# RWKV-7 layer on one core: key-query products on four array quarters, state outputs behind the chain of states, output stage in two parts

## Chip, cores and metric

The kernel runs on one core of a Trainium2 chip. The metric is the device time of one execution in microseconds (us); the time given for a kernel is the median of its runs. The core has TensorE (PE in the rows; PEld is its weight load), VectorE (DVE), ScalarE (ACT), GpSimd (POOL) and SyncE (SP), each with a queue of its own that it works off in order.

## The reference, cut to what matters

Two layers. The first mixes tokens with RWKV-7 heads (12 heads of 64, 2048 tokens), the second with differential attention; both attend to 256 memory tokens beside that, and an output projection follows each. The change is in the first layer alone, in this recurrence and what surrounds it:

```python
def step(state, inp):
    r_t, w_t, k_t, v_t, kk_t, a_t = inp
    sa = jnp.einsum('bhvk,bhk->bhv', state, -kk_t)
    state = (state * w_t[:, :, None, :]
             + sa[..., None] * (kk_t * a_t)[:, :, None, :]
             + v_t[..., None] * k_t[:, :, None, :])
    y_t = jnp.einsum('bhvk,bhk->bhv', state, r_t)
    return state, y_t
...
y = ((y - mean) * lax.rsqrt(var + LNX_EPS)).reshape(B, S, BR_W) * lnx_w + lnx_b
bonus = jnp.sum(r * k * r_k, axis=-1, keepdims=True) * v
return y + bonus.reshape(B, S, BR_W)
```

The caller multiplies the result by a SiLU gate.

## The kernel before

The recurrence is computed in chunks of 64 tokens. A step takes one pair of heads (128 columns) and a block of 512 tokens, which is eight chunks. There are 24 steps: two halves of the tokens, six pairs of heads, two blocks. The methods of a step:

- `p1`: the projections of the pair (`pj`, 24 matmuls of 128x128x512 each, for the keys kx, the receptances rx and the values vx, L174), the decay and its running sum (two `lr` products for the decay cum and two for asg, L317 and L318), the token shift (`mix`, three VectorE operations, L277 to L279), and the norm of the keys (`pss`, L335, which needs kk from kx).
- `p2`: key-query products `pg` (L371) of each chunk and head, masked into Gm (L373); transposes `bkp` and `pvt`; the bonus.
- `p3`: VectorE inverts 16x16 and 32x32 blocks of a triangular matrix by substitution (itmp and Ti alternate, L418 and L420), brings them with stream transposes into T and TT (L427, L431). `p3b`: TensorE doubles the blocks (`inv` L446, `invz` L459, `invr` L465).
- `gate`: projection and SiLU of the gate (L282 to L288).
- `p4`: the products that give each chunk's transition matrix MT and the rest (`atp`, `nvp`, `txp`, `mrp`, and `ch<-UV,BKT` L530).
- `p4b`: the chain of states. Eight links `ch<-S,MT` (L541), each followed by a copy to S on ScalarE (L542), which the next link reads; the first reads the state sb of the block before. The outputs `yp` come in part from inside a chunk (L550) and in part from the state (L555), two matmuls to a chunk, each of which needs that chunk's S.
- `p5`: VectorE normalises ys (bn_stats bs L564, a few small operations sm, L574 and L575), TensorE transposes it (`py`, L578), ScalarE scales (L580), VectorE adds the bonus (L581), GpSimd gates (L582) and stores to y_dram (L583).

The program is written in the order of a software pipeline: in turn i it holds p2 and p3 of step i+1, p4b and p5 of step i, p3b and p4 of step i+1, and then the gate of step i+1 and p1 of step i+2. A scheduler takes this program and sets the order of instructions on each engine, so pj of a later step stands between the links of the chain and in other places as a filler. The PSUM pool for pg, bkp, yp, py and the inverses has three buffers that go round; pj has three of its own.

Of the kernel before, what the change touches and what calls it, by code (L numbers as in the profile page):

```python
# [59 lines left out]
def hybrid_kernel(ctx, tc, S, HALF, x, mem, pv, cv, dist, postn, w_out, w_mkv, a_w, w2, a2, w_kv, b_w, out):  # L60
# [148 lines left out]
    def layer_a(ph):  # L209
# [64 lines left out]
        def mix(ps, col, o):  # L274
            m = pc("mu", col)
            A.activation(o, ps, AF.Copy, scale=omu[:, col:col + 1])
            V.scalar_tensor_tensor(out=o[:, 1:TB], in0=ps[:, 0:TB - 1], scalar=m, in1=o[:, 1:TB], op0=ALU.mult, op1=ALU.add)  # L277
            V.scalar_tensor_tensor(out=o[:, 0:1], in0=carry[:, col:col + 1], scalar=m, in1=o[:, 0:1], op0=ALU.mult, op1=ALU.add)
            V.tensor_copy(out=carry[:, col:col + 1], in_=ps[:, TB - 1:TB])  # L279

        def gate_silu(ps, g, eng=G_):
            A.activation(g, ps, AF.Copy)  # L282
            e = W([P, TB], "e_sil")
            A.activation(e, g, AF.Exp, scale=-1.0)
            V.tensor_scalar(out=e, in0=e, scalar1=BIG, scalar2=None, op0=ALU.min)
            A.activation(e, e, AF.Ln, bias=1.0)
            A.activation(e, e, AF.Exp, scale=-1.0)
            eng.tensor_tensor(out=g, in0=g, in1=e, op=ALU.mult)  # L288
            return g
# [13 lines left out]
        class Step:  # L303
# [5 lines left out]
            def p1(self):  # L309
# [5 lines left out]
                for i, e in enumerate((cum[:, :, 1:65], asg.rearrange("p (c t) -> p c t", t=C))):  # L315
# [3 lines left out]
                    A.activation(e, pl.rearrange("p (c t) -> p c t", t=C), AF.Exp, bias=nwa[:, i * 6 + p:i * 6 + p + 1], scale=-1.0)  # L319
                    V.tensor_scalar(out=e, in0=e, scalar1=BIG, scalar2=None, op0=ALU.min)  # L320
                    A.activation(e, e, AF.Ln, bias=1.0)
# [40 lines left out]
            def p2(self):  # L362
                p, AR, BK = self.p, self.AR, self.BK
                Gm = T([P, 2, NJ, 2, P], "Gm", 2)
                for e in range(2):

                    pgs = [PS([P, NJ, P], "pg") for hh in range(2)]
                    for j in range(NJ):
                        for hh in range(2):
                            hs = slice(hh * 64, hh * 64 + 64)  # L370
                            mm(pgs[hh][:, j, :], lhsT=BK[hs, 2 * j + e, :], rhs=AR[hs, 2 * j + e, :], start=True, stop=True)  # L371
                    for hh in range(2):
# [160 lines left out]
            def p4b(self):  # L533
# [6 lines left out]
                for c in range(NC):  # L540
                    mm(ch[:, c, :], lhsT=MT[:, c, :], rhs=st[c], start=False, stop=True, skip_group_check=True)  # L541
                    A.activation(st[c + 1], ch[:, c, :], AF.Copy, scale=PC[:, c:c + 1])  # L542
# [3 lines left out]
                for hh in range(2):  # L546
                    for j in range(NJ):
                        for e in range(2):
                            rr = hcs[e]
                            mm(py[hh][rr, j, :], lhsT=Gm[:, e, j, hh, rr], rhs=UV[:, 2 * j + e, hcs[hh]], start=j == 0, stop=False, skip_group_check=True)  # L550
                for j in range(NJ):
                    for e in range(2):
                        for hh in range(2):
                            c, rr = 2 * j + e, hcs[e]
                            mm(py[hh][rr, j, :], lhsT=RT[hcs[hh], c, :], rhs=st[c][hcs[hh]], start=False, stop=True, skip_group_check=True)  # L555
                for hh in range(2):
                    A.activation(ys[:, :, hh], py[hh], AF.Copy)

            def p5(self):
                p, ys, sil = self.p, self.ys, self.sil  # L560
                bs = T([P, 8, 6], "bs", 1)
# [12 lines left out]
                V.tensor_tensor(out=y8, in0=y8, in1=sm[:, 0, :, None].broadcast_to([P, 8, 64]), op=ALU.subtract)  # L574
                V.tensor_tensor(out=y8, in0=y8, in1=sm[:, 3, :, None].broadcast_to([P, 8, 64]), op=ALU.mult)  # L575
                py = PS([P, NJ, P], "py")
                for j in range(NJ):
# [115 lines left out]
        for i in range(n):  # L693
# [11 lines left out]
            if i + 1 < n:  # L705
                steps[i + 1].p3b()
                steps[i + 1].p4()
            if i + 2 <= n:
                filler(i + 2)
# [614 lines left out]
```

## Time and profile before

| what | value |
|---|---|
| median of 3 runs | 3177.18 us (3177.15 to 3179.72) |
| the profiled execution, its own time | 3178.13 us |
| span of the profile | 3176.3 us |
| TensorE busy | 2965.9 us, 93% |
| VectorE, ScalarE, GpSimd busy | 1792.0, 1508.2, 873.6 us |
| mean granted clock of TensorE | 0.97 |

The steps of the first layer run up to about 1480 us of the span. A stretch is the time from the first pg matmul of one step to the first of the next; stretches are counted from 0, and stretch 6 and 7 are shown most below. In rows of a timeline the columns are the start, the time from first start to last end, the engine, line, operation, what it writes and reads, its sizes, how many matmul passes it holds (a 32-bit matmul is recorded as two), and in brackets the engine's idle time before it with what ended it.

### The profile page before, as it was taken

What the parts mean: (1) busy time and instruction counts of PE and PEld (TensorE: products, weight loads), DVE (VectorE), ACT (ScalarE), POOL (GpSimd) and SP (SyncE); (2) the same over time, 40 slices, a digit from 0 to 9 for tenths busy, and PEclk for the clock granted to TensorE, in tenths of its full rate; (3) what the DMA queues carried; (4) which work ended last, traced back from release to release, by engine and by line L of the source; (5) the groups of instructions that cost most, each with busy time, mean ns of one, the idle gap of its engine ahead of it and who ended that gap; (6) DMA issues with size and microseconds to landing.
All of it is one profiled execution on the core that took longest, in us unless ns stands there. A gap on an engine that the chain in (4) does not pass through costs nothing.

```text
span 3176.3 us, 57448 instructions
## 1 busy us (share of the span) xinstructions
PE 2965.9 (93%) x22378; PEld 2401.6 (76%) x22378; DVE 1792.0 (56%) x4728; ACT 1508.2 (47%) x3318; POOL 873.6 (28%) x936
## 2 busy tenths in 40 slices
PE   6889999998789999998899999999999999998999
PEld 4667777776667777777677798898887787786777
DVE  6566767655656676764465311101108888887554
ACT  5535454444444544444455422313216777776343
POOL 3133433442134334431000222412312223222100
PEclk8999999998789999999999999999999999999999
DMA  3211000122110001103554523423454556533453
GB/s 118 80 30 36 28 23 26 35 77 79 36 33 28 23 26 33 38 25 86 164 145 126 155 80 99 118 83 87 117 158 110 114 112 120 116 80 108 121 156 115
DMA packets 266160, 265.45 MB, mean 84 GB/s; under 512 B 16832, under 2 KB 206656, under 8 KB 265760
## 3 DMA queue, kind: packets, MB, share of 16 engines
q1 hardware_dynamic: 237760, 195.31, 21.0%
q0 software_dynamic: 28128, 66.46, 10.3%
q8 instruction: 176, 2.88, 0.4%
q14 instruction: 96, 0.79, 0.1%
HBM read 180.45 MB, written 81.26 MB: 82 GB/s over the span
## 4 chain that ended last, share of the span: by engine, by line
PE 71%; DVE 13%; ACT 8%; issue 3%; DMA 3%; POOL 1%; SPq 1%; ACTq 0%; DVEq 0%; POOLq 0%
PE pj L174 28%; PE po L866 10%; PE o L1179 5%; PE vps L1042 4%; PE s L1138 3%; PE s L1139 2%; PE tr L1169 2%; DMA wraw<-in_a_w 2%; PE inv L446 2%; PE yp L555 1%; PE ch L541 1%; PE mo L805 1%; DVE E L1141 1%; PE mpt L798 1%; PE pss L335 1%
## 5 line engine op out<-in xcount | busy, mean ns | idle before, releaser
L174 PE MATMUL pj<-hhi,wh 128*128 128x512 f32 x928 | 396.3, 427 | 7.8 <-ACT sil L282 2.6
L174 PE MATMUL pj<-hhi,wl 128*128 128x512 f32 x928 | 379.4, 409 | 1.3 <-POOL wl L123 1.3
L174 PE MATMUL pj<-hlo,wh 128*128 128x512 f32 x928 | 373.9, 403 | 0.2 <-DVE hlo L149 0.2
L123 POOL TENSOR_TENSOR wl<-wraw,wh 128x512 fp32r<-128x512 f32 x168 | 220.0, 1320 | 431.5 <-ACT wh L122 378.0
L1141 DVE CUSTOM_DVE_ANT_0 E<-s,dist 128x512 f32<-128x512 f32 (+1 forms) x480 | 276.0, 604 | 35.2 <-PE s L1139 29.0
L174 PE MATMUL pj<-bh,wh 128*128 128x512 f32 x672 | 262.4, 391 | 0.0
L174 PE MATMUL pj<-bh,wl 128*128 128x512 f32 x672 | 262.3, 390 | 0.0
L174 PE MATMUL pj<-bl,wh 128*128 128x512 f32 x672 | 262.2, 390 | 0.0
L1146 ACT ACTIVATE E<-E,nm 128x1920 f32<-128x1920 f32 (+7 forms) x192 | 229.4, 1199 | 59.0 <-DVE nm L1144 58.6
L174 PEld LDWEIGHTS pj<-hhi,wh 128*128 128x128 f32 x928 | 179.2, 193 | 64.7 <-ACT sil L282 8.9
L122 ACT ACTIVATE wh<-wraw 128x512 fp32r<-128x512 f32 x168 | 105.2, 627 | 231.3 <-PE pj L174 143.6
L1179 PE MATMUL o<-th,vs 128*128 128x256 f32 (+1 forms) x864 | 210.9, 376 | 2.4 <-ACT th L1172 0.9
L174 PEld LDWEIGHTS pj<-hlo,wh 128*128 128x128 f32 x928 | 179.7, 194 | 41.7 <-issue 6.8
L174 PEld LDWEIGHTS pj<-hhi,wl 128*128 128x128 f32 x928 | 178.6, 192 | 42.0 <-POOL wl L123 2.2
L1138 PE MATMUL s<-ks,qd 128*128 128x512 f32 (+1 forms) x480 | 205.7, 432 | 2.2 <-DVE mx L1141 1.2
L1179 PEld LDWEIGHTS o<-th,vs 128*128 128x128 f32 x864 | 153.9, 189 | 38.5 <-ACT th L1172 19.2
L1139 PE MATMUL s<-ks,qd 128*128 128x512 f32 (+1 forms) x480 | 176.2, 373 | 0.0
L174 PEld LDWEIGHTS pj<-bh,wh 128*128 128x128 f32 x672 | 126.6, 188 | 26.3 <-DVE ot L877 0.3
L174 PEld LDWEIGHTS pj<-bh,wl 128*128 128x128 f32 x672 | 126.5, 188 | 26.3
L174 PEld LDWEIGHTS pj<-bl,wh 128*128 128x128 f32 x672 | 126.5, 188 | 25.9
L764 POOL DMA_DIRECT2D mq<-mq x64 | 33.3, 526 | 376.0 <-PE ms L783 368.3
L1172 ACT ACTIVATE th<-tr 128x512 f32<-128x512 f32 (+1 forms) x216 | 113.2, 568 | 44.2 <-PE tr L1169 43.8
(416 smaller groups left out, 7112.1 us busy)
## 6 DMA issues: line engine op xcount, KB each, us to landing
wraw<-in_a_w SPq DMA_DIRECT2D x126, 256.0 KB, 2.9
qd<-qd_d POOLq DMA_DIRECT2D x48, 512.0 KB, 7.0
mq<-mq POOLq DMA_DIRECT2D x64, 256.0 KB, 4.3
ks<-ks_d POOLq DMA_DIRECT2D x24, 512.0 KB, 7.2
yr<-y_dram SPq DMA_DIRECT2D x31, 384.0 KB, 5.0
xt<-in_x SPq DMA_DIRECT2D x16, 512.0 KB, 5.3
x_dram<-ot SPq DMA_DIRECT2D x16, 512.0 KB, 4.2
wraw<-in_b_w SPq DMA_DIRECT2D x32, 256.0 KB, 3.1
```

What stands on the lines that cost most here:

```text
L122: A.activation(hi[:, ks], raw, AF.Copy)
L123: eng.tensor_tensor(out=lo[:, ks], in0=raw, in1=hi[:, ks].bitcast(F32), op=ALU.subtract)
L174: mm(ps, lhsT=w[a_][:, k, wcol], rhs=h[b_][:, k, tsl], start=n == 0, stop=n == 3 * KT - 1)
L446: mm(pb[rows, j, hh, :], lhsT=lt[rows, j, hh, :], rhs=rt_[rows, j, hh, :], start=True, stop=True)
L866: mm(po[hf], lhsT=a_[:, k, :], rhs=b_[hf][:, k, :], start=k == i == 0, stop=k == KT - 1 and i == 2)
L1042: mm(ps[:, t, :], lhsT=hT[b][a_][:, k, tsl], rhs=w[b_][:, k, :], start=n == 0, stop=n == 3 * KT - 1)
L1138: mm(ps[:, f:f + w_], lhsT=qd[:, 0, c, qs], rhs=k_[:, c, 0:w_], start=True, stop=False)
L1139: mm(ps[:, f:f + w_], lhsT=qd[:, 1, c, qs], rhs=k_[:, c, 0:w_], start=False, stop=True)
L1141: V.tensor_tensor_reduce(out=e[:, kb * 512:kb * 512 + w], in0=ps[:, 0:w], in1=dt_[:, u0:u0 + w], scale=-SLOPES[h], scalar=3.0e38, op0=ALU. ...
L1146: A.activation(E[c][:, 0:nk], E[c][:, 0:nk], AF.Exp, bias=nm[:, c:c + 1], scale=-1.0, accum_out=nm[:, 2 + c:3 + c])
L1172: A.activation(th[:, 0:w], ps[:, 0:w], AF.Copy)
L1179: mm(po[:, oc], lhsT=vs[kt // 4][:, kt % 4, :], rhs=th[:, rc], start=n == 0, stop=n >= nmm - 2, skip_group_check=True)
```

## The change

Four edits. The key-query products of a chunk and head are split in two by output rows, so each reads 64 key rows, 64 columns of weights, and writes to one of four quarters; there are 32 matmuls where there were 16. The state outputs of a step are issued behind the last matmul of its chain. p5 ends with the normalised ys; transposes, scaling, bonus, gate and store are a method p5b, called between p3b and p4 of the next step (for the last step right behind p5). And the VectorE operations of the token shift, and the clamp in two sigmoids, have high priority for the scheduler.

```diff
--- before.py
+++ after.py
@@ -274,15 +274,17 @@
         def mix(ps, col, o):
             m = pc("mu", col)
             A.activation(o, ps, AF.Copy, scale=omu[:, col:col + 1])
-            V.scalar_tensor_tensor(out=o[:, 1:TB], in0=ps[:, 0:TB - 1], scalar=m, in1=o[:, 1:TB], op0=ALU.mult, op1=ALU.add)
-            V.scalar_tensor_tensor(out=o[:, 0:1], in0=carry[:, col:col + 1], scalar=m, in1=o[:, 0:1], op0=ALU.mult, op1=ALU.add)
-            V.tensor_copy(out=carry[:, col:col + 1], in_=ps[:, TB - 1:TB])
+            with tc.high_priority():
+                V.scalar_tensor_tensor(out=o[:, 1:TB], in0=ps[:, 0:TB - 1], scalar=m, in1=o[:, 1:TB], op0=ALU.mult, op1=ALU.add)
+                V.scalar_tensor_tensor(out=o[:, 0:1], in0=carry[:, col:col + 1], scalar=m, in1=o[:, 0:1], op0=ALU.mult, op1=ALU.add)
+                V.tensor_copy(out=carry[:, col:col + 1], in_=ps[:, TB - 1:TB])
 
         def gate_silu(ps, g, eng=G_):
             A.activation(g, ps, AF.Copy)
             e = W([P, TB], "e_sil")
             A.activation(e, g, AF.Exp, scale=-1.0)
-            V.tensor_scalar(out=e, in0=e, scalar1=BIG, scalar2=None, op0=ALU.min)
+            with tc.high_priority():
+                V.tensor_scalar(out=e, in0=e, scalar1=BIG, scalar2=None, op0=ALU.min)
             A.activation(e, e, AF.Ln, bias=1.0)
             A.activation(e, e, AF.Exp, scale=-1.0)
             eng.tensor_tensor(out=g, in0=g, in1=e, op=ALU.mult)
@@ -317,7 +319,8 @@
                     mm(pl, lhsT=lora[:, i], rhs=th[i], start=True, stop=False)
                     mm(pl, lhsT=lora[:, 2 + i], rhs=th[i], start=False, stop=True)
                     A.activation(e, pl.rearrange("p (c t) -> p c t", t=C), AF.Exp, bias=nwa[:, i * 6 + p:i * 6 + p + 1], scale=-1.0)
-                    V.tensor_scalar(out=e, in0=e, scalar1=BIG, scalar2=None, op0=ALU.min)
+                    with tc.high_priority():
+                        V.tensor_scalar(out=e, in0=e, scalar1=BIG, scalar2=None, op0=ALU.min)
                     A.activation(e, e, AF.Ln, bias=1.0)
                     A.activation(e, e, AF.Exp, scale=-1.0)
                 kx = W([P, TB], "kx")
@@ -366,9 +369,11 @@
 
                     pgs = [PS([P, NJ, P], "pg") for hh in range(2)]
                     for j in range(NJ):
-                        for hh in range(2):
-                            hs = slice(hh * 64, hh * 64 + 64)
-                            mm(pgs[hh][:, j, :], lhsT=BK[hs, 2 * j + e, :], rhs=AR[hs, 2 * j + e, :], start=True, stop=True)
+                        for d in range(2):
+                            for hh in range(2):
+                                o = hh ^ d
+                                hs, os_ = slice(hh * 64, hh * 64 + 64), slice(o * 64, o * 64 + 64)
+                                mm(pgs[hh][os_, j, :], lhsT=BK[hs, 2 * j + e, os_], rhs=AR[hs, 2 * j + e, :], start=True, stop=True)
                     for hh in range(2):
                         V.tensor_tensor(out=Gm[:, e, :, hh, :], in0=pgs[hh], in1=cc(("maskE", "maskO")[e], 128)[:, None, :].broadcast_to([P, NJ, P]), op=ALU.mult)
 
@@ -538,7 +543,7 @@
                 S = T([P, NC, C], "S", 1)
                 st = [sb[self.p][:, b % 2]] + [S[:, c] for c in range(1, NC)] + [sb[self.p][:, 1 - b % 2]]
                 for c in range(NC):
-                    mm(ch[:, c, :], lhsT=MT[:, c, :], rhs=st[c], start=False, stop=True, skip_group_check=True)
+                    last = mm(ch[:, c, :], lhsT=MT[:, c, :], rhs=st[c], start=False, stop=True, skip_group_check=True)
                     A.activation(st[c + 1], ch[:, c, :], AF.Copy, scale=PC[:, c:c + 1])
                 ys = self.ys = T([P, NJ, 2, C], "ys", 1)
 
@@ -548,16 +553,17 @@
                         for e in range(2):
                             rr = hcs[e]
                             mm(py[hh][rr, j, :], lhsT=Gm[:, e, j, hh, rr], rhs=UV[:, 2 * j + e, hcs[hh]], start=j == 0, stop=False, skip_group_check=True)
-                for j in range(NJ):
-                    for e in range(2):
-                        for hh in range(2):
-                            c, rr = 2 * j + e, hcs[e]
-                            mm(py[hh][rr, j, :], lhsT=RT[hcs[hh], c, :], rhs=st[c][hcs[hh]], start=False, stop=True, skip_group_check=True)
+                with tc.issue_after(last.ins):
+                    for j in range(NJ):
+                        for e in range(2):
+                            for hh in range(2):
+                                c, rr = 2 * j + e, hcs[e]
+                                mm(py[hh][rr, j, :], lhsT=RT[hcs[hh], c, :], rhs=st[c][hcs[hh]], start=False, stop=True, skip_group_check=True)
                 for hh in range(2):
                     A.activation(ys[:, :, hh], py[hh], AF.Copy)
 
             def p5(self):
-                p, ys, sil = self.p, self.ys, self.sil
+                ys = self.ys
                 bs = T([P, 8, 6], "bs", 1)
                 y8 = ys.rearrange("p j h v -> p (j h) v")
                 for i in range(8):
@@ -573,6 +579,9 @@
                 A.activation(sm[:, 3], sm[:, 3], AF.Exp, scale=-0.5)
                 V.tensor_tensor(out=y8, in0=y8, in1=sm[:, 0, :, None].broadcast_to([P, 8, 64]), op=ALU.subtract)
                 V.tensor_tensor(out=y8, in0=y8, in1=sm[:, 3, :, None].broadcast_to([P, 8, 64]), op=ALU.mult)
+
+            def p5b(self):
+                p, ys, sil = self.p, self.ys, self.sil
                 py = PS([P, NJ, P], "py")
                 for j in range(NJ):
                     nc.tensor.transpose(py[:, j, :], ys[:, j].rearrange("p h v -> p (h v)"), ident)
@@ -704,7 +713,11 @@
             steps[i].p5()
             if i + 1 < n:
                 steps[i + 1].p3b()
+                if True:
+                    steps[i].p5b()
                 steps[i + 1].p4()
+            if False or i + 1 == n:
+                steps[i].p5b()
             if i + 2 <= n:
                 filler(i + 2)
             if i == n - 2:
```

The built programs show what becomes of the order. TensorE, in the chain of stretch 6 (ch is a link, yp the outputs, pj a filler). Before, from its first link:

```order
L541 MATMUL ch<-sb_122,MT 128x64
L550 MATMUL yp<-UV,Gm 64x64 x16
L555 MATMUL yp<-sb_122,RT 64x64 x2
L541 MATMUL ch<-S,MT 128x64
L555 MATMUL yp<-S,RT 64x64 x2
L174 MATMUL pj<-hhi,wh 128x512
L174 MATMUL pj<-hlo,wh 128x512
L541 MATMUL ch<-S,MT 128x64
L555 MATMUL yp<-S,RT 64x64 x2
L174 MATMUL pj<-hhi,wl 128x512
L541 MATMUL ch<-S,MT 128x64
```

With the change, the end of the same chain:

```order
L546 MATMUL ch<-S,MT 128x64
L174 MATMUL pj<-hhi,wh 128x512
L174 MATMUL pj<-hlo,wh 128x512
L546 MATMUL ch<-S,MT 128x64
L174 MATMUL pj<-hhi,wl 128x512
L174 MATMUL pj<-hhi,wh 128x512
L546 MATMUL ch<-S,MT 128x64
L561 MATMUL yp<-sb_122,RT 64x64 x2
L561 MATMUL yp<-S,RT 64x64 x14
L174 MATMUL pj<-hlo,wh 128x512
L174 MATMUL pj<-hhi,wl 128x512
L174 MATMUL pj<-hhi,wh 128x512
```

The two yp matmuls of a link are gone from between the links, two pj stand in each, and the state outputs come as one block behind the last link.

TensorE at the end of stretch 6, where mrp ends one step's p4 and pss belongs to p1 of a later step. Before:

```order
L519 MATMUL mrp<-BKT,Wn 64x64
L520 MATMUL mrp<-Gm,Wn 64x64
L530 MATMUL ch<-UV,BKT 64x64 x16
L335 MATMUL pss<-rn,cvt 128x512
L174 MATMUL pj<-hhi,wh 128x512
L174 MATMUL pj<-hlo,wh 128x512
L174 MATMUL pj<-hhi,wl 128x512
```

With the change, behind `ch<-UV` and six more pj:

```order
L174 MATMUL pj<-hhi,wl 128x512
L174 MATMUL pj<-hhi,wh 128x512
L174 MATMUL pj<-hlo,wh 128x512
L174 MATMUL pj<-hhi,wl 128x512
L546 MATMUL ch<-sb_124,MT 128x64
L546 MATMUL ch<-S,MT 128x64 x2
L338 MATMUL pss<-rn,cvt 128x512
L174 MATMUL pj<-hhi,wh 128x512
L174 MATMUL pj<-hlo,wh 128x512
```

Ten pj, the last of the projection of kx, and the first three links of the next chain moved to between `ch<-UV` and pss. This order stands so at eleven places with the change (at the ends of the even stretches, from stretch 2 on, in stretch 10 with two links), and at two before (in stretches 12 and 13).

ScalarE at the same place with the change (S is the copy of a link, rn<-kk what pss reads; before, kx, Pt, cum and rn<-kk stand ahead of and among the copies of atp, nvp and txp):

```order
L512 ACTIVATE UV<-txp 64x2x128 x2
L122 ACTIVATE wh<-wraw 128x512
L276 ACTIVATE kx<-pj,omu 128x512
L331 ACTIVATE Pt<-cum 128x520
L547 ACTIVATE S<-ch,PC 128x64
L332 ACTIVATE cum<-cum 128x520
L547 ACTIVATE S<-ch,PC 128x64
L122 ACTIVATE wh<-wraw 128x512
L336 ACTIVATE rn<-kk 128x512
L547 ACTIVATE S<-ch,PC 128x64
L340 ACTIVATE rn<-rn 128x512
```

Copies of links stand between the steps from kx to rn, and kx behind the last copy of txp.

VectorE in stretch 7, up to T and TT, which inv reads. Before:

```order
L420 TENSOR_TENSOR Ti<-Ti,itmp 128x15
L568 TENSOR_TENSOR sm<-bs 128x8
L569 SCALAR_TENSOR_TENSOR sm<-sm 128x8
L425 TENSOR_SCALAR X_5227<-Ti,cvt 128x16x16 x2
L570 TENSOR_TENSOR sm<-sm 128x8
L571 TENSOR_SCALAR sm<-sm 128x8
L427 STREAM_TRANSPOSE T_5230<-X_5227 128x16x32
L429 TENSOR_SCALAR X_5226<-Ti,cvt 128x16x16 x2
L574 TENSOR_TENSOR ys<-ys,sm 128x512
L431 STREAM_TRANSPOSE TT_5234<-X_5226 128x16x32
L575 TENSOR_TENSOR ys<-ys,sm 128x512
L285 TENSOR_SCALAR e_sil<-e_sil 128x512
```

With the change:

```order
L425 TENSOR_TENSOR Ti<-Ti,itmp 128x2x14
L580 TENSOR_TENSOR ys<-ys,sm 128x512
L423 TENSOR_TENSOR itmp<-Dd,Ti 128x15
L581 TENSOR_TENSOR ys<-ys,sm 128x512
L425 TENSOR_TENSOR Ti<-Ti,itmp 128x15
L430 TENSOR_SCALAR X_5355<-Ti,cvt 128x16x16 x2
L432 STREAM_TRANSPOSE T_5358<-X_5355 128x16x32
L434 TENSOR_SCALAR X_5354<-Ti,cvt 128x16x16
L287 TENSOR_SCALAR e_sil<-e_sil 128x512
L434 TENSOR_SCALAR X_5354<-Ti,cvt 128x16x16
L323 TENSOR_SCALAR cum<-cum 128x8x64
L436 STREAM_TRANSPOSE TT_5362<-X_5354 128x16x32
```

Both large operations on ys moved ahead of X and T, and clamps (e_sil, cum) stand between X and TT. Earlier in that stretch the second M_ moved behind the last two Gm and bon, and GpSimd's rkb ahead of its two E; in even stretches those two orders change little. py now stands within or behind invr on TensorE, and four lr are split in even stretches, two ahead of inv and two behind it.

## Rows read from the trace of the kernel before

**Rows 1.** Page, part 1: busy time, share of the span, instructions.

```profile
PE 2965.9 (93%) x22378; PEld 2401.6 (76%) x22378; DVE 1792.0 (56%) x4728; ACT 1508.2 (47%) x3318; POOL 873.6 (28%) x936
```

**Rows 2.** Windows: stretch, length; busy of PE, PEld, DVE, ACT, POOL; clock; DMA.

```profile
430.96:480.51 49.55, 47.00 (x537) 37.49 (x537) 36.32 (x93) 24.26 (x53) 20.21 (x20) 1.00 0.09 28
480.51:531.55 51.04, 47.00 (x536) 37.65 (x536) 33.48 (x93) 23.70 (x52) 19.95 (x20) 1.00 0.10 30
905.31:966.06 60.75, 52.76 (x539) 42.02 (x539) 36.55 (x93) 24.29 (x53) 19.12 (x19) 0.89 0.07 22
```

**Rows 3.** Timeline of TensorE, chain of stretch 7 and the fillers behind it.

```profile
490.27 0.33 PE L555 MATMUL yp<-S,RT 64*64 64x64 f32 x4
490.53 0.51 PE L174 MATMUL pj<-hhi,wl 128*128 128x512 f32 x1
...
495.64 0.40 PE L174 MATMUL pj<-hlo,wh 128*128 128x512 f32 x1
495.88 0.39 PE L174 MATMUL pj<-hhi,wl 128*128 128x512 f32 x1
```

**Rows 4.** Timeline of TensorE, pg of stretch 7.

```profile
480.51 2.02 PE L371 MATMUL pg<-AR,BK 64*128 64x128 f32 x24
483.72 1.16 PE L371 MATMUL pg<-AR,BK 64*128 64x128 f32 x8 [1.18 <-DVE carry L279]
```

**Rows 5.** Waits (total, times, longest; 120 to 1480 us), and TensorE's timeline in stretch 7.

```profile
PE py L578 <- DVE ys L575: 20.6, 20, 2.3
...
503.81 0.63 PE L578 MATMUL py<-cvt,ys 128*128 128x128 f32 x4 [1.30 <-DVE ys L575]
...
514.94 1.75 PE L504 MATMUL txp<-X,TT 64*64 64x128 f32 x28 [0.48 <-ACT X L495]
```

**Rows 6.** Timeline of VectorE up to T, in stretches 7 and 8.

```profile
495.87 0.23 DVE L564 BATCH_NORM_STATS2 bs<-ys 128x6 f32<-128x64 f32 x1 [1.59 <-ACT ys L557]
...
498.97 1.08 DVE L427 STREAM_TRANSPOSE T<-X 128x512 f32<-128x512 f32 x1
...
501.20 0.68 DVE L574 TENSOR_TENSOR ys<-ys,sm 128x512 f32<-128x512 f32 x1
...
502.71 0.94 DVE L575 TENSOR_TENSOR ys<-ys,sm 128x512 f32<-128x512 f32 x1
...
538.60 1.43 DVE L409 TENSOR_SCALAR Dd<-M__5780,cvt 128x256 f32<-128x256 f32 x1
...
549.12 1.07 DVE L427 STREAM_TRANSPOSE T<-X 128x512 f32<-128x512 f32 x1
```

**Rows 7.** Timelines of TensorE and ScalarE at the end of stretch 12.

```profile
886.20 0.33 PE L541 MATMUL ch<-sb,MT 128*128 128x64 f32 x2
888.16 0.43 PE L541 MATMUL ch<-S,MT 128*128 128x64 f32 x2 [1.63 <-ACT S L542]
889.00 0.69 PE L541 MATMUL ch<-S,MT 128*128 128x64 f32 x2 [0.41 <-ACT S L542]
891.07 2.07 PE L335 MATMUL pss<-rn,cvt 128*128 128x512 f32 x2 [1.38 <-ACT rn L333]
...
889.87 0.63 ACT L122 ACTIVATE wh<-wraw 128x512 fp32r<-128x512 f32 x1 [0.92 <-DMA wraw<-in_a_w]
```

**Rows 8.** Timeline of TensorE in stretch 1, and windows behind three waits.

```profile
199.09 1.68 PE L446 MATMUL inv<-T,E 64*64 64x64 f32 x32 [4.01 <-DVE T L427]
...
199.50:202.90 3.40, 3.40 (x34) 2.44 (x31) 1.71 (x4) 2.66 (x5) 1.38 (x3) 0.50 0.13 39
...
502.50:505.90 3.40, 2.10 (x39) 1.84 (x39) 2.70 (x6) 1.87 (x4) 0.61 (x1) 1.00 0.38 106
...
889.00:895.80 6.80, 5.42 (x11) 3.62 (x12) 1.29 (x2) 2.61 (x5) 1.79 (x2) 0.50 0.31 86
```

**Rows 9.** Timeline of TensorE in stretch 6.

```profile
454.17 1.15 PE L446 MATMUL inv<-T,E 64*64 64x64 f32 x32
...
468.45 1.12 PE L335 MATMUL pss<-rn,cvt 128*128 128x512 f32 x2
```

## Prediction

> **What bounds the kernel now.** I read the busy times first: TensorE works 93% of the span [rows 1], so the question is what it does and what it waits for. In layer A the same 24 steps follow each other, and I cut the span at each step's first pg matmul. Stretches of even steps last 49.55 us and odd ones 51.04, both with 47.0 us of TensorE work at full clock; only stretch 13 stands out with 60.75 us at 0.89 [rows 2]. So each pair of stretches has 6.6 us of waits, and the rest is work. Everything behind layer A keeps its order on every engine, so the forecast is a sum over these stretches. I then read three timelines: TensorE through one chain of states [rows 3], VectorE up to T, which the inverse waits for [rows 6], and a place where chain links already stand with nothing between them [rows 7]. Positions below are us behind the stretch's first pg.
>
> **Key-query products.** The first 24 of the 32 rows of pg take 2.02 us, then TensorE waits 1.18 us for VectorE, whose first Gm frees a buffer, and the last 8 rows take 1.16 [rows 4]. Today two products on the two row halves run beside each other; each streams 128 columns. After the change four run beside each other, each streams 128 columns too, and there are twice as many. Work per streamed column is halved, the number doubled: I take 0. Bounds: if the quarters gave half the time, only the part behind the wait would gain, 0.5 us a step or 12 us in 24; if they ran only in pairs it would cost about 1.1 us again, 26 us. The Trainium skill, page "TensorEngine Tiling (Array Packing)", Theoretical Speedup, promises up to twice the speed where a free dimension is 64 or less; by it the time would be 12 us below my forecast. No row shows a 64-column stationary with 128 moving columns on four quarters. The Trainium skill's same page, Instruction Overhead, which sets a fixed cost on each matmul, speaks against it.
>
> **State outputs behind the chain.** Today one pair of yp matmuls stands in each link and costs 0.26 us (490.27 until the filler at 490.53), 8 a step [rows 3], or 2.1 us. Behind the chain they are one block of 32 rows. inv, 32 rows of the same size without a break, takes 1.15 us [rows 9], on two quarters of the array; the outputs go to all four, so I take 0.6 and a gain of 1.5 a step, between 1.0 (as inv) and 1.7. Only pj stand behind the block on TensorE, and the step's ys comes earlier, since the chain does. The links themselves need TensorE and ScalarE in turn; without cover one takes 0.84 us [rows 7], and with two pj between (0.23 us each [rows 3] and about 0.1 at each entry) it is covered just so: cost 0.
>
> **Output stage in two parts.** py now stands behind invr, so its waits for ys go: 20.6 us in 20 places, 1.30 in an odd stretch [rows 5], so some 0.8 in an even one. txp's wait for X, 0.48 a step [rows 5], goes too, since the transposes of py stand beside the same ScalarE work only later. The DMA of y leaves later with the gate behind it on GpSimd; its reader comes after layer A, so it costs nothing, and the last step keeps its old place.
>
> **What is late next: T.** The inverse (inv) needs T from VectorE. Less now stands ahead of inv on TensorE, so T becomes the last thing to arrive.
> *Even stretch.* inv started at 23.2 (454.17 [rows 9]). Ahead of it go 1.5 (outputs), 1.35 (py's 0.55 and its wait), 0.5 (two lr, each of two matmuls as long as a pj, now stand behind it) and 13 pj now placed behind it, 2.95; 0.3 goes with fewer changes between small and wide products. TensorE is there at 16.6. T started at 17.6, took 1.07 [rows 6] and stays where it is: ready at 18.6. Wait 2.0, inv at 18.6, 4.6 earlier.
> *Odd stretch.* inv started at 23.85 (py at 23.3 and 0.55 [rows 5]). Ahead of it go 1.5 (outputs), 1.85 (py), three links moved into the stretch before (0.8), four pj (0.9) and 0.8 of changes and short waits: TensorE is there at 18.0. T was ready at 19.5 (498.97 and 1.08 [rows 6]). In its new order VectorE no longer stops 1.59 us for ys, but both large ys operations (0.68 and 0.94 [rows 6]) and some sm stand ahead of X and T: 1.9; and the first itmp starts 1.2 later by my count, because M_ waits for two Gm and bon, and Dd then meets GpSimd's E, as in an even stretch, where Dd took 1.43 us [rows 6]. T is ready at 21.0: wait 3.0, inv 2.85 earlier.
>
> **What is late at the end of an even stretch.** The last ten pj of kx now stand behind ch<-UV, then come three links and pss. pss needs kx to go through ScalarE, VectorE (mix, kk) and ScalarE (rn). Nothing on TensorE covers that. The same order exists twice in the trace of before: from ch<-sb (886.20) to pss (891.07) it took 4.87 us, 0.92 of it a wait for weights [rows 7]; I take 3.9, of which 0.8 is the moved links' own work. Bounds 3.1 (if kx does not stand behind wh on ScalarE) and 4.9. It comes at ten more even stretches; in stretch 13 it is gone.
>
> **Sum of a warm stretch.** Even: -4.6 up to inv; behind it +0.5 lr, +0.55 py, +2.95 pj, -0.5 txp, +3.9 at the end: **+2.8**. From pss to the next pg nothing changes (12.06 us, 468.45 [rows 9]). Odd: -2.85; behind inv +0.9 pj, +0.55 py, -0.5 txp, and +0.6 because TT now stands behind two min operations: **-1.3**. A pair is 1.5 longer, without the clock.
>
> **The clock.** After the bare links at 886 the granted clock was 0.50 for 6.8 us, with 5.42 us of work in it: 2.7 us lost. After a wait of 4.01 us for T it was 0.50 for 3.4 us: 1.7 lost. After py's 1.30 it stayed at 1.00 [rows 8]. I take 2.2 for the end of an even stretch, 0 for the even wait for T (2.0, nearest to 1.30), and 1.0 for the odd one (3.0, between 1.30 and 4.01).
> Even 10 x (2.8 + 2.2) = +50; odd 9 x (-1.3 + 1.0) = -3; stretch 13 becomes an odd one and loses its low clock, from 60.75 to about 51.5 with small parts of the change of half: -9; stretches 11 and 12, which have the gains and no new stall, -3. **Sum +35 us.** The profiled execution took 3178.1, about 1 above the median of the runs, so the forecast against the median is **3212 us**. The edits in high priority move short VectorE operations (0.1 to 0.75 us); what they do is in the order above, so they have no price of their own.
>
> **Rivals.**
> *The clock holds.* Waits between small matmuls could be too short for a fall. Against: both rows of long waits are followed by 0.50 [rows 8]. Time: 10 x 2.8 - 9 x 1.3 - 12 = +4, 3181 us, no change.
> *T is in time.* If M_ and Dd are not held by E and ys comes late enough to let X pass, both waits for T go, with the odd clock: even 0.8 + 2.2, odd -4.3: +30 - 39 - 12 = -21, **3156 us**, faster. It decides once T is ready before 17 in both. For: half of the delay is placed by order, not by a measured row. Against: the even T already started at 17.6.
> *The end of the even stretch is covered.* If kx passes in the time of the links (0.84 each), 3.1 and the clock go: even -0.3, odd -0.3, -12: -18, 3159 us, faster. Against: the place in [rows 7], where the same links stood.
> *Clock falls fully at both* (2.7 and 1.7): 10 x 5.5 + 9 x 0.4 - 12 = +47, 3224 us.
> *pg does what four quarters could:* half the time, -12 on the forecast, 3200 us, still slower; or pairs only, +26, 3238 us.
>
> **How the numbers follow.** Forecast 0.50; full clock 0.12; pg halves 0.03; pg doubles 0.04; the clock holds 0.13; T in time 0.10; covered end 0.08. Measurement can tell about 0.2%, some 6.4 us. Faster: 0.10 + 0.08 = 0.18. Same: 0.13. Slower: 0.69. The range goes from 3165, which leaves out the two faster cases (0.18), to 3238, the worst pg.
>
> **What would show it.** Right: PE's idle before inv put down to T, about 2.0 in even and 3.0 in odd stretches; some 3 us of idle between ch<-sb and pss at ten places, each followed by a granted clock of 0.50; py without a wait; pg with the same length in twice the rows; even stretches near 54.5, odd near 51. Wrong: even stretches under 50, T ready before 17, a clock of 1.00 behind the bare links, or pg's last rows well under 1.08 us.

## The result, and the profile after the change

The changed kernel takes 3211.9 us (median of 4 runs, 3209.6 to 3213.0), 1.0112 times the time before (95% interval 1.0094 to 1.0129): 35 us slower, as forecast (3212). The profiled execution has a span of 3211.2 us at a mean granted clock of 0.961; before it was 3176.3 us at 0.970.

Windows of the changed kernel: stretch 6, stretch 7 and stretch 13, which answer to [rows 2], and two windows on low clocks inside stretches 6 and 7. The columns are those of [rows 2].

```profile
441.65:494.97 53.32, 48.30 (x575) 36.79 (x574) 36.10 (x93) 25.15 (x57) 19.74 (x20) 0.97 0.09 27
494.97:547.47 52.50, 47.30 (x563) 36.70 (x562) 35.23 (x93) 22.84 (x49) 19.72 (x20) 0.93 0.10 28
923.69:977.55 53.86, 47.95 (x563) 36.85 (x562) 36.40 (x93) 22.73 (x49) 19.20 (x19) 0.94 0.08 24
481.20:484.60 3.40, 2.96 (x5) 1.73 (x6) 0.70 (x2) 0.71 (x3) 1.22 (x1) 0.51 0.47 138
515.10:521.90 6.80, 5.25 (x54) 4.22 (x55) 3.64 (x9) 3.81 (x7) 1.93 (x3) 0.51 0.21 57
```

The even stretch went from 49.55 to 53.32 us, the odd one from 51.04 to 52.50, and stretch 13 from 60.75 to 53.86. In both kinds the clock fell: for 3.4 us at the end of the even one and for 6.8 us around inv in the odd one, with 2.96 and 5.25 us of work in it. It does not fall alike everywhere. Stretches 16 and 18 hold the same matmuls in the same order, with the same waits to within 0.03 us up to pss:

```profile
1083.38:1138.33 54.95, 49.90 (x575) 37.91 (x574) 35.64 (x93) 25.16 (x57) 19.69 (x20) 0.94 0.10 29
1190.37:1242.37 52.00, 46.97 (x576) 36.10 (x575) 36.09 (x93) 25.04 (x56) 19.33 (x20) 1.00 0.09 27
```

Behind the bare links of stretch 16 the clock is 0.50 for 6.8 us, behind those of stretch 18 it stays at 1.00. Of the ten even stretches from 2 on that end with bare links only with the change, six have the low clock for 3.4 us, two (16 and 20) for 6.8 and two (18 and 22) not at all.

TensorE's timeline of stretch 6, which answers to [rows 4], [rows 7] and [rows 9]:

```profile
441.65 1.74 PE L376 MATMUL pg<-AR,BK 64*64 64x128 f32 x42
444.26 1.09 PE L376 MATMUL pg<-AR,BK 64*64 64x128 f32 x22 [0.87 <-DVE Gm L378]
...
459.87 1.15 PE L451 MATMUL inv<-T,E 64*64 64x64 f32 x32 [1.16 <-DVE T L432]
...
474.33 1.15 PE L535 MATMUL ch<-UV,BKT 128*64 128x64 f32 x32
...
477.81 0.33 PE L546 MATMUL ch<-sb,MT 128*128 128x64 f32 x2
479.77 0.43 PE L546 MATMUL ch<-S,MT 128*128 128x64 f32 x2 [1.63 <-ACT S L547]
480.61 0.43 PE L546 MATMUL ch<-S,MT 128*128 128x64 f32 x2 [0.41 <-ACT S L547]
481.64 2.07 PE L338 MATMUL pss<-rn,cvt 128*128 128x512 f32 x2 [0.60 <-ACT rn L336]
```

pg is as long as before with twice the rows (two row halves took 1.82 and 1.16 us in the even stretch before, four quarters take 1.74 and 1.09). inv stands at 18.2 us and has waited 1.16 for T. From ch<-sb to pss it takes 3.83 us with 2.64 of idle time in three pieces.

Stretch 7, which answers to [rows 5] and [rows 6]:

```profile
512.63 0.50 PE L174 MATMUL pj<-hhi,wh 128*128 128x512 f32 x1 [1.19 <-ACT sil L283]
...
516.65 1.98 PE L451 MATMUL inv<-T,E 64*64 64x64 f32 x32 [2.59 <-DVE X L434]
...
527.16 0.66 PE L587 MATMUL py<-cvt,ys 128*128 128x128 f32 x4
...
535.51 1.12 PE L338 MATMUL pss<-rn,cvt 128*128 128x512 f32 x2
```

TensorE waits 1.19 us for the gate's copy and then 2.59 for T (the row names X of L434, which VectorE starts as T ends); inv starts at 21.7. py behind invr waits for nothing. Over all steps, from the list of waits (us in total, times, longest):

```profile
PE inv L451 <- DVE X L434: 27.1, 10, 3.9
PE inv L451 <- DVE T L432: 19.8, 12, 4.4
```

Summed over the stretches of both traces, one window for each: the nine regular even stretches are 35.4 us longer together and stretch 10 another 4.2; eight regular odd ones 5.3; stretches 11 and 12 are 5.4 shorter, stretch 13 is 6.9 shorter; stretches 0 and 1 are 2.3 longer, and what lies ahead of the first pg and from the last step on changes by less than 0.1. That is 34.9, the difference of the two spans.

### The profile page after: what moved, and what is told of

Its sections match the earlier page's. It is cut to its first block, busy times and chain, and to the rows that moved or that the text cites. A ratio compares the mean times of both kernels' runs of the same rounds, so it can differ in the third digit from the quotient of the medians.

```text
span 3211.2 us, 58965 instructions
## 1 busy us (share of the span) xinstructions
PE 2962.1 (92%) x23146; PEld 2371.8 (74%) x23146; DVE 1810.2 (56%) x4728; ACT 1507.1 (47%) x3318; POOL 866.9 (27%) x936
## 4 chain that ended last, share of the span: by engine, by line
PE 69%; DVE 17%; ACT 7%; issue 3%; DMA 2%; POOL 0%; SPq 0%; ACTq 0%; DVEq 0%; POOLq 0%
PE pj L174 30%; PE po L879 9%; PE o L1192 5%; PE vps L1055 4%; PE s L1151 3%; PE s L1152 2%; DVE Ti L425 2%; PE inv L451 2%; DVE itmp L423 2%; PE tr L1182 2%; DVE Gm L378 2%; PE pss L338 1%; PE mo L818 1%; DVE E L1154 1%; PE mpt L811 1%
## 5 line engine op out<-in xcount | busy, mean ns | idle before, releaser
L174 PE MATMUL pj<-hlo,wh 128*128 128x512 f32 x928 | 382.4, 412 | 0.0
L1154 DVE CUSTOM_DVE_ANT_0 E<-s,dist 128x512 f32<-128x512 f32 (+1 forms) x480 | 276.1, 604 | 35.4 <-PE s L1152 29.4
L1192 PEld LDWEIGHTS o<-th,vs 128*128 128x128 f32 x864 | 154.1, 189 | 38.1 <-ACT th L1185 18.8
```

The costliest lines, as they stand in the source:

```text
L174: mm(ps, lhsT=w[a_][:, k, wcol], rhs=h[b_][:, k, tsl], start=n == 0, stop=n == 3 * KT - 1)
L1154: V.tensor_tensor_reduce(out=e[:, kb * 512:kb * 512 + w], in0=ps[:, 0:w], in1=dt_[:, u0:u0 + w], scale=-SLOPES[h], scalar=3.0e38, op0=ALU. ...
L1192: mm(po[:, oc], lhsT=vs[kt // 4][:, kt % 4, :], rhs=th[:, rc], start=n == 0, stop=n >= nmm - 2, skip_group_check=True)
```

## Experiments

The theory to be tested (A): VectorE's T sets when the inverse starts, so what TensorE saves ahead of it turns into waiting; the late kx sets the end of the even stretch; both come with the output stage in two parts. Its rival (B): every edit brings its own term, which add up.

### One edit at a time

*Output stage in two parts alone* (the call of the second part between p3b and p4 of the next step, nothing else):

```diff
             steps[i].p5()
             if i + 1 < n:
                 steps[i + 1].p3b()
+                steps[i].p5b()
                 steps[i + 1].p4()
```

> Of the four edits only the output stage in two parts. Theory A (the split does it: it puts both large ys operations ahead of T on VectorE and the last pj of kx and three links between ch<-UV and pss on TensorE): T and pss stand as late as with all four edits, and what the state outputs cost again is swallowed by the wait for T, so about 3212 us (3204 to 3222), with bare links in front of pss at eleven places. Theory B (every edit brings its own term): the 1.5 us a step that the state outputs gained come back, 24 x 1.5 = 36, so about 3248 us. Theory C (the loss comes from the other edits): within 10 us of 3177.

Measured: 3196.2 us, ratio 1.0053 (1.0038 to 1.0068). That is outside all three. TensorE's timeline of its stretch 6:

```profile
462.17 1.15 PE L449 MATMUL inv<-T,E 64*64 64x64 f32 x32 [0.24 <-DVE T L430]
...
481.52 0.43 PE L544 MATMUL ch<-S,MT 128*128 128x64 f32 x2 [1.63 <-ACT S L545]
482.36 0.43 PE L544 MATMUL ch<-S,MT 128*128 128x64 f32 x2 [0.41 <-ACT S L545]
483.40 1.13 PE L338 MATMUL pss<-rn,cvt 128*128 128x512 f32 x2 [0.60 <-ACT rn L336]
```

inv stands 18.8 us behind pg (443.40) instead of 18.2, and waits 0.24 for T instead of 1.16: if that is the outputs, which stand in the links again, they cost 0.6 of their 1.5 us here and the rest had been waiting (two more edits are left out in this run). The bare links are there with the same 2.64 us of idle time. So the mechanism of A stands, and the split alone brings both waits. The size does not: in this stretch the granted clock stays at 1.00 through the links, in others it falls, and the stretches lie between 49.7 and 56.2 us.

*All but the split*:

```diff
             steps[i].p5()
+            steps[i].p5b()
             if i + 1 < n:
                 steps[i + 1].p3b()
-                steps[i].p5b()
                 steps[i + 1].p4()
```

> The changed kernel with the output stage in one part again. Theory A: in stretches 0 to 11 pss has no bare links before it and T is not behind ys, so these lose nothing and gain at most 1 to 2.5 us each (py still waits for ys, which VectorE finishes at the same time); in stretches 14 to 22 the scheduler places four links without a filler in front of something else, which costs some 3 us each; about 3185 us (3160 to 3205). Theory B: the terms of the other three edits without the split's, 3177 - 36 = 3141 us.

Measured: 3268.7 us, 1.0279 (1.0264 to 1.0295), the slowest of all, and a miss for both. The list of waits:

```profile
PE py L587 <- DVE ys L581: 42.1, 20, 3.1
PE invz L464 <- DVE Ta L457: 32.4, 19, 4.2
PE ch L546 <- ACT S L547: 29.0, 43, 1.6
```

py's wait has doubled against [rows 5], and invz waits where it hardly did (5.1 us in total before), since 23 pj stand ahead of py in the order and hardly one between the steps of the inverse, and links stand bare in the second half. The split costs when it is alone and saves 57 us beside the three others.

*State outputs behind the chain alone* (`with tc.issue_after(last.ins):` around the state outputs):

> Only the state outputs behind the chain. Theory A: VectorE finishes ys for py at about 22.5 us behind pg whatever the chain does, so py just waits longer and the 1.5 us a step are swallowed; only the two to eight more pj that stand ahead of py are gained, 0.5 to 0.9 us a step: 3155 to 3172 us, more if the longer wait lets the clock fall. Theory B: the 1.5 us a step are on the path: 3141 us.

Measured: 3217.8 us, 1.0125 (1.0104 to 1.0146). Waits and two rows of TensorE's timeline, stretches 6 and 7:

```profile
PE py L585 <- DVE ys L579: 47.5, 20, 3.6
...
460.98 0.63 PE L585 MATMUL py<-cvt,ys 128*128 128x128 f32 x4 [1.80 <-DVE ys L579]
...
513.42 0.69 PE L585 MATMUL py<-cvt,ys 128*128 128x128 f32 x4 [3.06 <-DVE ys L579]
```

py stands at 22.9 us in stretch 6, where it stood at 22.65 before; its waits went from 20.6 to 47.5 us. The saving was swallowed entirely, as A says; and in the odd stretches the wait is now 3.06 us and the clock is 0.50 up to 517.2, which makes the whole slower than before. The expectation named that fall, but not its size.

*Four quarters alone*:

> Only the key-query products on four quarters. Theory A (four run beside each other where two did, twice as many): 0, so 3172 to 3182 us, and the rows of pg take as long as before. Theory D (the quarters give twice the speed): 0.5 us a step behind the wait for Gm, 3165 us. Theory E (only pairs run beside each other): 3203 us.

Measured: 3191.8 us, 1.0041 (1.0026 to 1.0057). TensorE's timeline of stretch 7, and one wait:

```profile
488.08 1.71 PE L376 MATMUL pg<-AR,BK 64*64 64x128 f32 x42
491.12 1.09 PE L376 MATMUL pg<-AR,BK 64*64 64x128 f32 x22 [1.33 <-DVE Gm L378]
...
512.26 0.63 PE L587 MATMUL py<-cvt,ys 128*128 128x128 f32 x4 [1.93 <-DVE ys L581]
...
PE txp L509 <- ACT X L500: 15.3, 18, 1.9
```

pg is no longer and no shorter. What is longer are the waits for py (1.93 in this stretch, before 1.30) and txp (15.3 us in total, before 8.3); the fillers stand in other places in this order. D and E fall; A's price for pg holds, its time for the kernel does not.

*High priority alone* (`with tc.high_priority():` around the token shift and the clamps):

> Only the high priority of the token shift's VectorE operations and the clamps. The order moves little: pss ahead of txp in even stretches, one more pj ahead of py. Theory A: VectorE ends ys for py later by the operations now ahead of it, 0 to 0.5 us a step: 3175 to 3192 us. Rival: no difference, 3172 to 3182.

Measured: 3195.0 us, 1.0062 (1.0039 to 1.0084), slightly above the range of A. The waits for py fell to 16.0 us, against A. What is longer are odd stretches of the first half: in 3, 5 and 9 the clock is 0.94, in 7 it is 0.97 (before 0.97, 1.00, 0.97 and 1.00). The low clock begins there about 4 us behind the first pg, where the second group of pg has waited 1.7 us (1.0 to 1.2 before). Whether this wait makes the clock fall no run shows.

Alone, the outputs, the split, the quarters and the priority cost some 38, 17, 12 and 15 us; together they cost 35. B falls: nothing adds up.

### Is it kx or the links that stall the end of the even stretch?

```diff
-                for c in range(NC):
-                    last = mm(ch[:, c, :], lhsT=MT[:, c, :], rhs=st[c], ...
+                with tc.issue_after(pssl[-1]):
+                    for c in range(NC):
+                        last = mm(ch[:, c, :], lhsT=MT[:, c, :], rhs=st[c], ...
```

> The changed kernel, with the links of a chain queued on TensorE behind pss, so that no link stands bare in front of it; ten pj of kx still stand between ch<-UV and pss. In the order, ys is no longer ahead of T in odd stretches and all eight links stand in each chain. Theory F (kx standing late makes the stall, the links only stand in it): pss waits about 2.9 us with nothing before it, now in both kinds of stretch, and the clock falls as before; even stretches 52 to 53, odd ones 51.5 to 52.5: 3190 to 3205 us. Theory G (the links and their copies on ScalarE make the stall): pss does not wait, even stretches near 49: about 3140 us.

Measured: 3245.1 us, 1.0211 (1.0194 to 1.0228). TensorE's timeline from stretch 6 on, and the wait in total:

```profile
489.46 1.12 PE L339 MATMUL pss<-rn,cvt 128*128 128x512 f32 x2 [3.23 <-ACT rn L337]
...
506.79 1.09 PE L378 MATMUL pg<-AR,BK 64*64 64x128 f32 x22 [2.02 <-DVE Gm L380]
...
PE pss L339 <- ACT rn L337: 73.1, 23, 4.7
```

(pssl holds the pss matmuls in the order of the program.) With no link ahead of it pss waits 3.23 us in even stretches and 2.94 in odd ones: kx's way over ScalarE and VectorE is the cause, the links only stood in it. F is right in its mechanism. It was too low by 40 us, since it left out that the second pg then waits 2.02 us and that the odd stretches, at a clock of 0.94, come to 56 us.

### Taking the late kx away

```diff
                     A.activation(e, e, AF.Exp, scale=-1.0)
+                yield
                 kx = W([P, TB], "kx")
...
+            f = None
+            if i + 2 <= n:
+                f = filler(i + 2)
+                next(f, None)
             if i + 1 < n:
                 steps[i + 1].p3b()
                 if True:
                     steps[i].p5b()
                 steps[i + 1].p4()
...
-            if i + 2 <= n:
-                filler(i + 2)
+            if f is not None:
+                list(f)
```

> The changed kernel, with the gate and the two lr of the step after next written ahead of the inverse, and the rest of p1 where it was. In the order, 17 and 21 pj stand between the two inv blocks, kx is done before txp, pss stands directly behind ch<-UV without links, and ys is behind T. Theory A (T on VectorE ends each stretch's first part, the late kx its last): the stall at the end goes (3.9 us and 1.3 of clock in each even stretch), T still makes inv wait 1.1 in even and about 2.4 in odd stretches: even near 48.5, odd near 50: about 3135 us (3115 to 3165). Rival H (TensorE's time, moved, only turns up as another wait on VectorE or ScalarE): within 10 us of 3212 or of 3177.

Measured: 3144.1 us, 0.989 (0.987 to 0.9911): faster than both kernels. Behind the gate and the two lr, filler and p1 pause (both are generators now), and go on where filler was called. Windows of stretches 6 and 7, and TensorE's timeline of both:

```profile
435.47:484.12 48.65, 45.70 (x569) 35.38 (x569) 36.34 (x93) 24.11 (x53) 19.80 (x20) 1.00 0.10 29
484.12:534.68 50.56, 45.96 (x569) 35.53 (x569) 35.92 (x93) 23.68 (x52) 19.47 (x20) 1.00 0.10 30
```

```profile
453.73 1.15 PE L452 MATMUL inv<-T,E 64*64 64x64 f32 x32 [0.74 <-DVE T L433]
...
470.95 1.15 PE L536 MATMUL ch<-UV,BKT 128*64 128x64 f32 x32
472.03 1.12 PE L339 MATMUL pss<-rn,cvt 128*128 128x512 f32 x2
...
510.27 1.15 PE L452 MATMUL inv<-TT,E 64*64 64x64 f32 x32 [1.16 <-ACT E L454]
```

pss follows ch<-UV without a gap, no clock falls in these stretches (stretches 3 and 13 are at 0.88), and they take 48.65 and 50.56 us, where 48.5 and 50 were expected. inv still stands at 18.26 and still waits for T: 0.74 us. 68 us go against the changed kernel, about as A worked out: kx is in time again, and in odd stretches T is there at 18.7 us instead of 21.5. T's place in even stretches has not moved.

The same with kx's projection ahead of the inverse too (`yield` behind `mix(pj(ws[0], h), 6 + p, kx)`):

> As the run before it, but the projection of kx too is written ahead of the inverse: 24 pj stand between lr and inv, so T is there before TensorE is in even stretches; in odd ones one matmul of inv stands ahead of them and waits for T. Theory A: even stretches have no wait for T and none for pss, near 47; odd ones wait 2.4 us at that single matmul, with the clock: near 50; about 3125 us (3100 to 3155). Rival H: the inverse has no filler left between its steps, its copies on ScalarE and VectorE show as 2 us and more of waits a stretch: 3170 us or above.

Measured: 3220.9 us, 1.0134 (1.0119 to 1.0149). H holds, for this version:

```profile
PE inv L452 <- ACT E L454: 58.8, 22, 4.3
```

24 pj ahead of inv cover T; then nothing is left to cover E's copy on ScalarE between the two inv blocks.

*Only the early writing, none of the four edits:*

> The kernel before with only the gate and the two lr written early, none of the four edits. py still stands ahead of inv and waits for ys, the bare links at the change of half stay. Theory A (the gain of p1_early needs py behind invr and the outputs behind the chain, which uncover T as the last thing): 3165 to 3190 us. Rival (the early p1 is the whole gain): about 3144 us.

Measured: 3205.5 us, 1.0089 (1.0072 to 1.0106): slower than the kernel before, and slower than A expected; most odd stretches take 56 us at 0.94. The early writing alone is not the gain; it needs the edits.

### Undoing single edits where the stall is gone

*State outputs back in the links*, otherwise as p1_early:

> The kernel of the run p1_early without its second edit: the state outputs stand in the links again. The rest of the order is the same but for a few pj in odd stretches. Theory A (T comes from VectorE at about 18.2 us in even stretches whatever TensorE does, so the 1.5 us of outputs only shorten the wait for T, 0.7 to 1.1 in even and about 2 in odd ones): 0.4 to 0.8 us a step in even stretches, 0 in odd ones, 3146 to 3158 us, with the wait of inv for T nearly gone in even stretches. Theory B (the outputs are on the path): 24 x 1.5 = 36 more, 3180 us.

Measured: 3188.0 us, 1.0036 (1.0022 to 1.0051). By the total B wins; the windows and the timeline of stretches 6 and 7 say otherwise:

```profile
439.66:488.49 48.83, 46.74 (x569) 37.31 (x569) 36.70 (x93) 23.89 (x53) 19.77 (x20) 1.00 0.10 29
488.49:543.23 54.74, 49.76 (x569) 39.66 (x569) 35.55 (x93) 23.90 (x52) 19.50 (x20) 0.94 0.10 28
```

```profile
458.44 1.15 PE L452 MATMUL inv<-T,E 64*64 64x64 f32 x32
...
516.31 1.15 PE L452 MATMUL inv<-TT,E 64*64 64x64 f32 x32 [1.79 <-ACT E L454]
```

The even stretch is 48.83 us, 0.18 more than with the outputs behind the chain, and inv, at 18.8, waits for nothing: so TensorE came 1.3 us later, of which 0.74 had been a wait for T. Of the 36 us between the two profiles, 33 are in the eight regular odd stretches and 2 in the even ones. In the odd ones the second inv waits 1.79 us for E (1.16 in p1_early), with 23 pj ahead of it instead of 21, and the clock is 0.50 from 518.8 on, where p1_early keeps 1.00. So A holds where the clock does, and the total came out as B's number by another way.

*Key-query products on two halves*, otherwise as p1_early:

> The kernel of the run p1_early without its first edit: key-query products on two row halves, 16 matmuls a step. Theory A: four quarters stream as many columns at a time, so nothing: 3139 to 3150 us, and the rows of pg take as long. Theory D (quarters are faster): 3150 us and more, up to 12 more. Theory E (they cost): under 3139.

Measured: 3148.4 us, 0.9907 (0.9892 to 0.9922), not distinguishable from p1_early. pg in its stretch 6:

```profile
429.22 1.83 PE L375 MATMUL pg<-AR,BK 64*128 64x128 f32 x22
431.64 1.16 PE L375 MATMUL pg<-AR,BK 64*128 64x128 f32 x10 [0.59 <-DVE Gm L377]
```

Even stretches are 48.46 us instead of 48.64, but this is no price of pg: inv stands at 18.25 in both kernels, and behind it the second inv waits for E in p1_early and not here. In p1_early:

```profile
459.20 1.15 PE L452 MATMUL inv<-TT,E 64*64 64x64 f32 x32 [0.22 <-ACT E L454]
```

Odd stretches go the other way: 51.5 to 53.2 us here, 50.6 in seven of eight with the quarters. The Trainium skill, page "TensorEngine Tiling (Array Packing)", Theoretical Speedup, gives up to twice the speed for a dimension of 64 or less. For this split, with 128 moving columns, the trace shows no such gain: 1.83 and 1.16 us on the halves, 1.74 and 1.09 on the quarters.

*No high priority*, otherwise as p1_early:

> The kernel of the run p1_early without its fourth edit, the high priority on VectorE. In the order pss stands ahead of txp and three more pj ahead of it in even stretches; the bare links come back in stretch 12. Theory A: that stretch costs about 6 us, the others the same: 3144 to 3158 us. Rival (the priority costs, as the run of it alone): 3128 to 3138 us.

Measured: 3177.7 us, 1.0005 (0.9989 to 1.0021), its runs between 3163 and 3187 us. Neither expectation: the priority saves some 33 us here and costs 15 alone. Stretch 12 is 5.2 us longer, near what A said. The profiled run is the fastest of ten, and shows only 14 of the 33 us: most even stretches differ by 0.4 us, and odd ones take 50.0 to 55.6, at clocks from 1.00 to 0.91, which makes 12 of the 14. For the slower runs this is not shown.

## Why the prediction was right, point by point

The forecast and the time agree within 1 us, and that is luck: even stretches brought 10 us less than forecast, odd ones 8 more, and stretch 0, which the sum left out, 2.5. The direction and the two stalls were right for reasons that the rows show, the late T of odd stretches was not.

- **Key-query products: right.** 0 was taken, and pg takes the same time. Neither the half nor the double came.
- **State outputs: right in size, and swallowed as the sum had it.** The block takes 0.7 us from 454.83 on (0.6 taken), and without it TensorE came to inv 1.3 us later in the run early_no_ia (1.5 taken). What it saves showed up as waiting for T, for py, or for E in the versions above.
- **py and txp: right.** Neither waits in the changed kernel.
- **T in even stretches: right in kind, over-sized.** TensorE came at 17.1 (16.6 forecast), T at 18.2 (18.6): a wait of 1.16, not 2.0.
- **T in odd stretches: near in size, wrong in its reason.** inv started at 21.7, 21.0 was forecast. TensorE came at 19.1 (18.0 forecast), since it had waited 1.19 for the gate, which the sum did not have; the wait for T was 2.59 (3.0). The sum made T 1.5 us later by the ys operations ahead of it and by a later first itmp. With the stop for ys gone these cancel: the last Ti starts at 17.44, and stood at 17.45 before. What makes T late is that this Ti and the X behind it took 0.17 and 0.73 us before, and take 1.27 and 1.71 in the new order, where GpSimd works on wl (the low part of the split weights) beside them. VectorE and GpSimd before, then with the change, in stretch 7:

```profile
498.21 0.73 DVE L425 TENSOR_SCALAR X<-Ti,cvt 128x256 f32<-128x256 f32 x2
499.58 1.28 POOL L123 TENSOR_TENSOR wl<-wraw,wh 128x512 fp32r<-128x512 f32 x1 [3.31 <-PE lr L318]
```

```profile
512.41 1.27 DVE L425 TENSOR_TENSOR Ti<-Ti,itmp 128x15 f32<-128x15 f32 x1
513.72 1.71 DVE L430 TENSOR_SCALAR X<-Ti,cvt 128x256 f32<-128x256 f32 x2
...
512.23 1.42 POOL L123 TENSOR_TENSOR wl<-wraw,wh 128x512 fp32r<-128x512 f32 x1 [5.28 <-ACT wh L122]
513.66 1.26 POOL L123 TENSOR_TENSOR wl<-wraw,wh 128x512 fp32r<-128x512 f32 x1
```

  These 2.1 us stand in every regular odd stretch of the changed kernel. With the split alone X takes 2.7 us beside wl; in p1_early, where wl starts behind X, it takes 0.73 and T is there at 18.7. No run moved wl by itself.
- **The end of the even stretch: right.** 3.83 us from ch<-sb to pss, 3.9 forecast, at the places that the order names. The run with links behind pss shows that it is kx.
- **A warm stretch: right.** Up to pss an even stretch grew by 2.5 us (pss at 40.0, before 37.5); 2.8 forecast. In stretch 7, pss came 1.5 us later, with the low clock around inv in it. What that clock costs shows in stretch 17, which has the same matmuls and the same wait, with a clock of 1.00 behind it:

```profile
1161.89 1.15 PE L451 MATMUL inv<-T,E 64*64 64x64 f32 x32 [2.58 <-DVE X L434]
...
1178.38 1.13 PE L338 MATMUL pss<-rn,cvt 128*128 128x512 f32 x2
```

  From inv to pss it takes 16.5 us there and 18.9 in stretch 7. Without these 2.4 us a warm odd stretch would be 0.9 shorter; 1.3 was forecast.
- **The clock: the two terms were mis-sized in opposite directions.** 2.2 us were put on the end of an even stretch and 1.0 on the wait in an odd one. Measured: 1.3 in stretch 6 (from pss to the next pg 13.33 instead of 12.06) and 2.4 in stretch 7. 1.3 is also the mean of the regular even stretches, which range from 0 (18 and 22) to 2.9 (16 and 20). So the even stretches brought 39.6 us where 50 were forecast, and the nine odd ones (with stretch 1) 5.1 where -3 was.
- **The odd stretch of before: a slip.** 51.04 us was taken for all. Four of the eight (3, 9, 19 and 21) take 52.5 to 52.7, at a clock of 0.97: it is 0.50 there for 3.4 us from about 4 us behind the first pg, where pg has waited 1.0 to 1.2 us, as it has in stretch 7 with a clock of 1.00. Against the mean of the eight the change in odd stretches is +0.7 us, for stretch 7 alone it is +1.5.
- **Stretches 11 to 13:** -12.3 together; -12 forecast (13: -6.9 for -9; 11 and 12: -5.4 for -3).
- **High priority: put at nothing, and not nothing.** Alone it costs 15 us; in p1_early it saves 33.

Of the rivals, "T is in time" and "the end is covered" are excluded by the rows above, "the clock holds" by the windows at 0.51, though it did hold at two of the ten even stretches. The premise that each edit has a price of its own failed: the experiments show prices that turn sign with the other edits, and in each of these orders fillers stand elsewhere.

What stays open: why the clock falls behind one pause and not behind another alike (2.64 us of idle time in the same three pieces, followed by 0.50 in stretch 16 of the changed kernel and by 1.00 in its stretch 18), and which wait makes it fall in the odd stretches of the runs with one edit.

## What to carry to other kernels

Where two engines take turns, follow the one that is waited for: of 1.3 us of TensorE's work a step, saved ahead of T, only 0.2 were left in the length of the even stretch. Look too at what other engines run beside the one that is waited for: VectorE's last two steps to T grew by 2.1 us beside GpSimd's wl. An edit in a scheduled kernel is first of all a new order, so read what stands in front of each wait (here the last ten projections of kx, and fillers gone from an inverse) before pricing the edit itself; moving one piece of the program by hand, the gate and lr ahead of the inverse, was worth 68 us against the changed kernel. And a pause is priced with a range for the low clock that may follow it: behind the same 2.64 us of idle time it cost from nothing to 2.9 us.

## What was not expected of the hardware

Four 64x64 quarters with 128 moving columns do the same products in the same time as two row halves (1.74 and 1.09 us against 1.82 and 1.16), with twice the instructions. The granted clock fell to 0.50 behind waits of 1.0 to 3.2 us, and did not fall behind others of that size (py's 1.80 us with the outputs behind the chain alone: it fell in stretch 4, not in 6); in runs that differ by a few matmuls odd stretches lie between 50.6 and 56 us. VectorE's two X operations took 0.73 us by themselves and 1.7 to 2.8 beside GpSimd's wl.
